# Taking the gathered expert slots of a unit in the order 0, 8, 1, 9 and so on

## The chip, the cores and the metric

The kernel runs on one core of a Trainium2 chip. Its engines are TensorE (PE, with its weight loads shown as PEld), VectorE (DVE), ScalarE (ACT), GpSimd (POOL) and SyncE (SP, which only issues DMAs). Each engine takes its own instructions in order and waits on semaphores. Sixteen DMA engines move data between the chip's memory (HBM) and the on-chip memory (SBUF). The metric is the device time of one execution in microseconds, as the median of the runs shown: 3331.66 us for the kernel before, from three runs between 3331.08 and 3334.54 us.

## The reference, cut to what matters

The reference computes two transformer blocks on 256 tokens of width 2048, in float32. The change lies in one part of the second block, a mixture of 16,384 tiny experts. Each of 8 heads of a token picks its 16 best experts. For each of them the row `u` is multiplied with the token, a gelu is taken, and the row `v` is added to the token's output with that weight:

```
top_s, top_i = lax.top_k(s, PEER_TOPK)                 # PEER_TOPK = 16, per half of the key
cand = top_s[..., 0, :, None] + top_s[..., 1, None, :]
best_s, best_c = lax.top_k(cand, PEER_TOPK)            # best first
experts = i1 * N_KEYS + i2
gates = jax.nn.softmax(best_s, axis=-1)
...
u = peer_u[ec]
act = jax.nn.gelu(jnp.einsum('tkd,td->tk', u, xc))
return jnp.einsum('tk,tkd->td', gc * act, peer_v[ec])
```

The 16 experts of a head are sorted, the best first, so their gates fall with the rank. With the inputs used here many gates of the later ranks are so small that the softmax gives zero in float32.

## The kernel before, in words

Nearly all of the program is dense matrix products whose weights stream in from HBM. The part in question, `peer` (L1318), stands between the second block's attention and recurrence and its last gated layer (`ple`).

*Units and slots.* The 256 tokens are cut into four blocks of 64 (`u`), the 8 heads into four pairs (`g`). A **unit** is one (`u`, `g`): partitions 0 to 63 hold the 64 tokens for the first head of the pair, partitions 64 to 127 the same tokens for the second. There are 16 units, and a unit has 16 **slots**, 256 in all. Slot `j` of a unit does this (`slot`, L1385):

- POOL issues one indirect DMA (L1389), which gathers into a buffer `uvb` one row per partition, 4096 floats (16 KiB): the expert's `u` row and `v` row, as the list `idx[:, j]` names them. An index beyond the table is skipped, and its row isn't fetched.
- DVE multiplies the `u` half with the tokens and sums (L1393, a SCALAR_TENSOR_TENSOR and the read of its accumulator).
- ACT takes the gelu, multiplies by the gate, and makes a diagonal matrix `dgs` (L1394 to L1397).
- PE multiplies that with the `v` half and adds it into `acc_e` (L1402).

There are six buffers `uvb` (`UVB`), used in turn. The gather of slot n+6 is issued when PE has read the buffer of slot n. DVE, ACT and PE take the slots in the order in which they are issued.

*The lists.* `route` (L1419) makes the 16 expert numbers and gates per partition for one unit, almost all on DVE. At its end it adds a large number to each expert number whose gate is zero, so that the gather skips that row. It also swaps the list's halves for partitions 64 to 127 (L1474): column `j` holds rank `j` in partitions 0 to 63, and rank `j`+8, or `j`-8 from column 8 on, in partitions 64 to 127. So slots 0 to 7 take the first head's ranks 0 to 7 beside the second head's ranks 8 to 15, and slots 8 to 15 the other way round. For unit 0 the first six columns (L1480 to L1482) get their expert numbers without skips, so that every buffer is filled once.

*The order of the work.* In `peer` the loop over slots calls `slot` and after every second one advances the next unit's `route` by a step; `route` has six such steps. The program text is not the order on an engine: a scheduler of the language places each engine's instructions by what it estimates, and it lets the routing run up to four units ahead (the lists have four buffers). On DVE the routing stands in bursts: most of units 1 to 4's in unit 0, and then one unit's at the turn of each unit, until the last unit's is done in unit 9.

The following lines are the functions that the change touches.

## Time and profile before

| | us |
|---|---|
| median of the runs | 3331.66 |
| the profiled execution | 3339.52 |
| its span, first to last instruction | 3337.8 |
| L1393 on DVE, 256 slots, busy | 586.3 |
| L1402 on PE, 256 slots, busy | 590.3 |
| L1389 on POOL, 256 gathers, busy | 432.6 |

The profile is one execution. Busy times are sums over an engine's instructions. A line of instructions shows how often it ran, its busy time, the mean of one, and the idle time of the engine just before it with the work that ended that idle time. Units are counted from 0, in the order (`u`, `g`). The slots run from 2253.3 us (the first gather's issue) to 3221.5 us (the last slot's matmuls end). Before and after them the program is dense products.

### The profile page before, as it was taken

How to read it: one execution, taken by the hardware profiler on the slowest of the kernel's cores; microseconds unless marked ns; L12 is line 12 of the kernel's file. 1: busy time of each engine (PE TensorE's matmuls, PEld its weight loads, DVE VectorE, ACT ScalarE, POOL GpSimd, SP SyncE). 2: the span in 40 equal slices, each digit the busy share in tenths (PEclk: the TensorE clock that was granted, in tenths of full speed). 3: DMA queues.
4: the chain of work that ended last, by engine and by line, in shares of the span. 5: the costliest groups of instructions: out<-in, count | busy, mean ns of one | idle time of the engine just before them, and what ended most of it. 6: DMA issues, size and time to landing. Idle time of an engine off the chain costs nothing. (4 is left out here: it accounts for less than half of the span.)

```text
span 3337.8 us, 45840 instructions
## 1 busy us (share of the span) xinstructions
PE 2918.3 (87%) x17372; PEld 2274.2 (68%) x17372; DVE 2165.0 (65%) x3087; ACT 1439.5 (43%) x2464; POOL 545.6 (16%) x320
## 2 busy tenths in 40 slices
PE   8999999999999999999999999985556666666678
PEld 8888888989898989999999998881111111111136
DVE  7769675545555555875445677559777867776755
ACT  5446655434343445664434445433222323222234
POOL 0000000000000000010000110003453444454511
PEclk9999999999999999999999999997897788899979
DMA  7645564666666666556665446637767767777864
GB/s 255 182 149 185 165 182 145 186 190 186 191 183 195 183 189 189 166 183 184 183 183 171 144 156 215 184 114 281 279 253 291 276 258 269 291 289 294 309 234 144
DMA packets 156397, 693.14 MB, mean 208 GB/s; under 512 B 34049, under 2 KB 36353, under 8 KB 139777
## 3 DMA queue, kind: packets, MB, share of 16 engines
q1 hardware_dynamic: 119312, 425.64, 41.8%
q0 software_dynamic: 36864, 264.57, 21.1%
q8 instruction: 137, 2.24, 0.3%
q14 instruction: 84, 0.69, 0.1%
HBM read 955.12 MB, written 4.19 MB: 287 GB/s over the span
## 5 line engine op out<-in xcount | busy, mean ns | idle before, releaser
L1402 PE MATMUL acc_e<-uvb,dgs 128*64 128x512 f32 x2048 | 590.3, 708 | 363.3 <-ACT dgs L1397 363.1
L1393 DVE SCALAR_TENSOR_TENSOR f<-uvb,xg 128x2048 bf16<-128x2048 f32 x256 | 586.3, 2290 | 229.2 <-DMA uvb<-in_uv,idx 219.2
L1402 PEld LDWEIGHTS acc_e<-uvb,dgs 128*64 128x64 f32 x2048 | 141.8, 154 | 801.8 <-ACT dgs L1397 610.3
L1389 POOL DMA_INDIRECT uvb<-in_uv,idx x256 | 432.6, 1690 | 753.7 <-PE acc_e L1402 408.8
L1394 ACT ACTIVATE act<-act 128x1 f32<-128x1 f32 x256 | 51.9, 203 | 638.6 <-DVE f L1393 638.5
L381 PE MATMUL acc_w_up<-f,l_w_up 128*128 128x256 f32 x1024 | 289.9, 283 | 0.0
L378 PE MATMUL acc_w_up<-f,h_w_up 128*128 128x256 f32 x1024 | 289.8, 283 | 0.0
L380 PE MATMUL acc_w_up<-f,h_w_up 128*128 128x256 f32 x1024 | 289.8, 283 | 0.0
L362 DVE TENSOR_TENSOR l_w_up<-r_w_up,h_w_up 128x1024 fp32r<-128x1024 f32 x128 | 165.8, 1295 | 175.7 <-PE acc_w_up L381 153.2
L362 DVE TENSOR_TENSOR l_w_down<-r_w_down,h_w_down 128x1024 fp32r<-128x1024 f32 x128 | 161.3, 1260 | 162.1 <-PE acc_w_down L372 133.4
L361 ACT CAST h_w_down<-r_w_down 128x1024 fp32r<-128x1024 f32 x128 | 135.1, 1055 | 197.8 <-PE acc_w_down L373 168.6
L361 ACT CAST h_w_up<-r_w_up 128x1024 fp32r<-128x1024 f32 x128 | 134.9, 1054 | 196.4 <-PE acc_w_up L380 175.4
L371 PE MATMUL acc_w_down<-h_w_down,f 128*128 128x512 f32 x512 | 199.6, 390 | 0.0
L372 PE MATMUL acc_w_down<-l_w_down,f 128*128 128x512 f32 x512 | 199.5, 390 | 0.0
L373 PE MATMUL acc_w_down<-h_w_down,f 128*128 128x512 f32 x512 | 199.2, 389 | 0.0
L380 PEld LDWEIGHTS acc_w_up<-f,h_w_up 128*128 128x128 f32 x1024 | 196.6, 192 | 0.1
L378 PEld LDWEIGHTS acc_w_up<-f,h_w_up 128*128 128x128 f32 x1024 | 196.6, 192 | 0.1
L381 PEld LDWEIGHTS acc_w_up<-f,l_w_up 128*128 128x128 f32 x1024 | 196.6, 192 | 0.0
L584 POOL TENSOR_TENSOR f<-f 128x1024 f32<-128x1024 f32 x16 | 30.3, 1896 | 802.7 <-ACT f L583 802.7
L373 PEld LDWEIGHTS acc_w_down<-h_w_down,f 128*128 128x128 f32 x512 | 96.1, 188 | 19.9
L372 PEld LDWEIGHTS acc_w_down<-l_w_down,f 128*128 128x128 f32 x512 | 96.1, 188 | 19.8
L371 PEld LDWEIGHTS acc_w_down<-h_w_down,f 128*128 128x128 f32 x512 | 96.1, 188 | 19.7
(555 smaller groups left out, 7818.0 us busy)
## 6 DMA issues: line engine op xcount, KB each, us to landing
r_w_up<-in_w_up SPq DMA_DIRECT2D x128, 512.0 KB, 3.7
r_w_down<-in_w_down SPq DMA_DIRECT2D x128, 512.0 KB, 4.2
r_w_qkv<-in_w_qkv SPq DMA_DIRECT2D x48, 512.0 KB, 3.6
r_w_xbc<-in_w_xbc SPq DMA_DIRECT2D x32, 512.0 KB, 4.5
r_w_xr<-in_w_xr SPq DMA_DIRECT2D x32, 512.0 KB, 3.6
r_w_yr<-in_w_yr SPq DMA_DIRECT2D x32, 512.0 KB, 3.6
r_w_gr<-in_w_gr SPq DMA_DIRECT2D x32, 512.0 KB, 3.6
r_w_ro<-in_w_ro SPq DMA_DIRECT2D x32, 512.0 KB, 3.7
```

Of the source, the lines that this page charges most:

```text
L361: nc.scalar.copy(wh, raw)
L362: nc.vector.tensor_sub(wl, raw, wh.bitcast(F32))
L371: nc.tensor.matmul(o, xh[:, s], h, start=first, stop=False)
L372: nc.tensor.matmul(o, xh[:, s], l, start=False, stop=False)
L373: nc.tensor.matmul(o, xl[:, s], h, start=False, stop=fin)
L378: nc.tensor.matmul(o, wh[:, s], xh, start=first and b % 2 == 0, stop=False, skip_group_check=True)
L380: nc.tensor.matmul(o, wh[:, s], xl, start=False, stop=False, skip_group_check=True)
L381: nc.tensor.matmul(o, wl[:, s], xh, start=False, stop=fin, skip_group_check=True)
L1389: nc.gpsimd.indirect_dma_start(out=b, out_offset=None, in_=self.ap["uv"], in_offset=bass.IndirectOffsetOnAxis(ap=idx[:, j:j + 1], axis=0), ...
L1393: nc.vector.scalar_tensor_tensor(junk, b[:, :D], 1.0, xg, op0=ALU.mult, op1=ALU.mult, accum_out=a[:, 0:1])
L1394: nc.scalar.activation(a[:, 2:3], a[:, 0:1], AF.Gelu_apprx_tanh)
L1402: nc.tensor.matmul(acc[i * 64:(i + 1) * 64, c * 512:(c + 1) * 512], dg, b[:, o:o + 512], start=first, stop=last)
```

## The change

The loop takes the columns of the list in the order 0, 8, 1, 9, 2, 10 and so on to 7, 15. Lists, gates, gathered rows and sums stay the same except in the very first six gathers. `first` and `last`, which open and close PE's accumulation, follow the place in the loop (`begin`, `end`). The steps of the next unit's `route` are called after places 0, 1, 3, 4, 6 and 7. In the first unit the six columns without skips are now 0 to 2 and 8 to 10, which takes four small casts in place of two.

```diff
+            order = [r + 8 * i for r in range(8) for i in range(2)]
...
-                for j in range(16):
-                    self.slot(u, g, j, uv[slot % UVB], xg[u], junk, acc[u])
+                for k, j in enumerate(order):
+                    self.slot(u, g, j, uv[slot % UVB], xg[u], junk, acc[u], k == 0, k == 15)
                     slot += 1
-                    if j % 2:
+                    if k in (0, 1, 3, 4, 6, 7):
                         next(later, None)
-                    if g == 0 and j == 2 and u:
+                    if g == 0 and k == 2 and u:
                         self.block_out(u - 1, acc[u - 1])
-                    if i == 15 and j in (3, 6, 9, 12):
-                        if j == 3:
+                    if i == 15 and k in (3, 6, 9, 12):
+                        if k == 3:
...
-        first, last = g == 0 and j == 0, g == 3 and j == 15
+        first, last = g == 0 and begin, g == 3 and end
...
-            nc.vector.tensor_copy(idx[0:64, :UVB], ids[0:64, 0, :UVB])
-            nc.vector.tensor_copy(idx[64:128, :UVB], ids[64:128, 0, 8:8 + UVB])
+            k = UVB // 2
+            for p, o in ((0, 0), (64, 8)):
+                nc.vector.tensor_copy(idx[p:p + 64, 0:k], ids[p:p + 64, 0, o:o + k])
+                nc.vector.tensor_copy(idx[p:p + 64, 8:8 + k], ids[p:p + 64, 0, 8 - o:8 - o + k])
```

How the instructions stand on an engine is shown at two places. The first is DVE at the start of unit 2 (`u` 0, `g` 2), in the kernel before; `act0_2_8` is the sum of slot column 8 of that unit, `tv`, `bc` and `tiu` are routing of later units:

```order
L1393 SCALAR_TENSOR_TENSOR f4_301_21719,act0_2_1_22286<-uvb3_21716,xg0_21709 128x2048
L1490 MAX tv23_24515<-sc23_24513 128x8 x2
L1491 MAX_INDEX bc21_24038<-best21_24037,cand21_24035 128x8
L1491 MAX_INDEX tiu23_24516<-tv23_24515,sc23_24513 128x8 x2
L1393 SCALAR_TENSOR_TENSOR f4_301_21719,act0_2_2_22314<-uvb4_21717,xg0_21709 128x2048
L1393 SCALAR_TENSOR_TENSOR f4_301_21719,act0_2_3_22327<-uvb5_21718,xg0_21709 128x2048
L1393 SCALAR_TENSOR_TENSOR f4_301_21719,act0_2_4_22346<-uvb0_21713,xg0_21709 128x2048
L1393 SCALAR_TENSOR_TENSOR f4_301_21719,act0_2_5_22359<-uvb1_21714,xg0_21709 128x2048
```

The same place on DVE in the changed kernel (its lines are numbered higher by up to three):

```order
L1394 SCALAR_TENSOR_TENSOR f4_301_21721,act0_2_8_22303<-uvb3_21718,xg0_21711 128x2048
L1493 MAX tv23_24504<-sc23_24502 128x8 x2
L1494 MAX_INDEX bc21_24014<-best21_24013,cand21_24011 128x8
L1494 MAX_INDEX tiu23_24505<-tv23_24504,sc23_24502 128x8 x2
L1394 SCALAR_TENSOR_TENSOR f4_301_21721,act0_2_1_22322<-uvb4_21719,xg0_21711 128x2048
L1394 SCALAR_TENSOR_TENSOR f4_301_21721,act0_2_9_22335<-uvb5_21720,xg0_21711 128x2048
L1394 SCALAR_TENSOR_TENSOR f4_301_21721,act0_2_2_22360<-uvb0_21715,xg0_21711 128x2048
L1394 SCALAR_TENSOR_TENSOR f4_301_21721,act0_2_10_22383<-uvb1_21716,xg0_21711 128x2048
```

The columns change, and the routing stays between the same places: from unit 1 on, each gap between two slots holds the same number of routing instructions in both kernels. Only unit 0 differs. There DVE in the kernel before has 16 routing instructions between the first two slots, 16 before the third and 12 before the fourth; the end of the first gap is this (`mr286`, `eq02` and `ex02` are routing):

```order
L1456 TENSOR_TENSOR eq020_22139<-ab02_22133,cst_75 128x256
L1456 TENSOR_TENSOR eq021_22169<-ab02_22133,cst_75 128x256
L1467 RECIPROCAL s286_22201<-s286_22201 128x1
L1492 MATCH_REPLACE mr286_22305<-tv03_22303,sc03_22301 128x128
L1393 SCALAR_TENSOR_TENSOR f4_301_21719,act0_0_1_21738<-uvb1_21714,xg0_21709 128x2048
L1458 TENSOR_TENSOR eq020_22139<-eq020_22139,tif02_22095 128x256
L1458 TENSOR_TENSOR eq021_22169<-eq021_22169,tif02_22095 128x256
L1468 TENSOR_SCALAR ex02_22199<-ex02_22199,s286_22201 128x16
```

In the changed kernel DVE has 39 there, then 2 and 5; the end of the first gap, with the next three slots:

```order
L1494 MAX_INDEX tiu11_22846<-tv11_22845,sc11_22843 128x8 x2
L1496 MAX best03_22349<-mr288_22351 128x8
L1394 SCALAR_TENSOR_TENSOR f4_301_21721,act0_0_8_21755<-uvb1_21716,xg0_21711 128x2048
L1497 MAX_INDEX bc03_22350<-best03_22349,mr288_22351 128x8
L1464 TENSOR_TENSOR ex03_22423<-best03_22349 128x16
L1394 SCALAR_TENSOR_TENSOR f4_301_21721,act0_0_1_21774<-uvb2_21717,xg0_21711 128x2048
L1451 TENSOR_SCALAR au03_22371<-bc03_22350 128x16
L1452 TENSOR_SCALAR au03_22371<-bc03_22350 128x16
L1467 TENSOR_REDUCE s290_22425<-ex03_22423 128x1
L1453 CAST ab03_22370<-au03_22371 128x32
L1468 RECIPROCAL s290_22425<-s290_22425 128x1
L1394 SCALAR_TENSOR_TENSOR f4_301_21721,act0_0_9_21787<-uvb3_21718,xg0_21711 128x2048
```

Routing that stood between the second and the fourth slot now stands between the first and the second; by the fourth slot the two sums are 44 and 46 instructions.

## Rows read from the trace of the kernel before

**Rows 1.** Page, costliest groups: line, shapes, count | busy us, mean ns | idle before, releaser.
```profile
L1402 PE MATMUL acc_e<-uvb,dgs 128*64 128x512 f32 x2048 | 590.3, 708 | 363.3 <-ACT dgs L1397 363.1
L1393 DVE SCALAR_TENSOR_TENSOR f<-uvb,xg 128x2048 bf16<-128x2048 f32 x256 | 586.3, 2290 | 229.2 <-DMA uvb<-in_uv,idx 219.2
L1389 POOL DMA_INDIRECT uvb<-in_uv,idx x256 | 432.6, 1690 | 753.7 <-PE acc_e L1402 408.8
```
**Rows 2.** Windows: unit 0, units 1 to 8, units 9 to 15: busy us, clock, DMA share, GB/s.
```profile
2261.54:2343.66 82.12, 46.17 (x168) 13.64 (x168) 80.68 (x272) 30.92 (x77) 30.03 (x16) 0.79 0.71 276
2343.66:2837.68 494.02, 302.22 (x1056) 74.60 (x1056) 373.38 (x627) 145.15 (x464) 217.11 (x129) 0.85 0.74 271
2837.68:3216.25 378.57, 244.91 (x884) 59.59 (x886) 261.20 (x248) 98.81 (x346) 179.04 (x106) 0.88 0.75 285
```
**Rows 3.** Line L1393 in units 1 to 8: count, ns min/median/max; DVE's idle by releaser.
```profile
L1393 DVE SCALAR_TENSOR_TENSOR f<-uvb,xg x128: 2271/2292/2307, 2343.7 to 2831.0; 128x2048 bf16<-128x2048 f32 x128
...
  DMA uvb<-in_uv,idx: 111.3, 66
```
**Rows 4.** Line L1393 in units 9 to 15: the same.
```profile
L1393 DVE SCALAR_TENSOR_TENSOR f<-uvb,xg x112: 2279/2293/2334, 2837.7 to 3216.2; 128x2048 bf16<-128x2048 f32 x112
...
  DMA uvb<-in_uv,idx: 107.3, 75
```
**Rows 5.** DMA queues of the page: packets, MB, share of 16 engines.
```profile
q0 software_dynamic: 36864, 264.57, 21.1%
```
**Rows 6.** Windows: the first gathers, a routing burst, and the last gathers.
```profile
2262.00:2285.00 23.00, 11.31 (x38) 3.44 (x40) 22.80 (x85) 9.89 (x22) 6.06 (x3) 0.72 1.01 430
3197.00:3216.00 19.00, 12.44 (x32) 2.65 (x30) 8.91 (x8) 3.38 (x12) 0.00 (x0) 0.60 0.24 96
...
2460.00:2476.00 16.00, 6.93 (x24) 1.51 (x22) 15.26 (x52) 6.17 (x16) 4.27 (x3) 0.89 0.54 213
```
**Rows 7.** DVE's timeline at the last slots: start us, us, instruction, idle before.
```profile
3201.62 2.29 DVE L1393 SCALAR_TENSOR_TENSOR f<-uvb,xg 128x2048 bf16<-128x2048 f32 x1 [2.61 <-DMA uvb<-in_uv,idx]
...
3216.25 2.29 DVE L1393 SCALAR_TENSOR_TENSOR f<-uvb,xg 128x2048 bf16<-128x2048 f32 x1 [2.58 <-DMA uvb<-in_uv,idx]
```
**Rows 8.** DVE's timeline in unit 2 and at the start of unit 3.
```profile
2417.72 2.29 DVE L1393 SCALAR_TENSOR_TENSOR f<-uvb,xg 128x2048 bf16<-128x2048 f32 x1
...
2420.05 2.29 DVE L1393 SCALAR_TENSOR_TENSOR f<-uvb,xg 128x2048 bf16<-128x2048 f32 x1
...
2431.21 2.29 DVE L1393 SCALAR_TENSOR_TENSOR f<-uvb,xg 128x2048 bf16<-128x2048 f32 x1 [1.86 <-DMA uvb<-in_uv,idx]
...
2459.65 2.29 DVE L1393 SCALAR_TENSOR_TENSOR f<-uvb,xg 128x2048 bf16<-128x2048 f32 x1 [1.36 <-DMA uvb<-in_uv,idx]
...
2475.76 2.27 DVE L1393 SCALAR_TENSOR_TENSOR f<-uvb,xg 128x2048 bf16<-128x2048 f32 x1
```
**Rows 9.** DVE's timeline before the first gather, one of the casts of L1481 and L1482.
```profile
2251.86 0.16 DVE L1481 CAST idx<-ids 64x6 uint32<-64x6 f32 x1
```
**Rows 10.** POOL's timeline in unit 2: gathers issued while DVE runs slot on slot.
```profile
2423.51 2.03 POOL L1389 DMA_INDIRECT uvb<-in_uv,idx  x1 [0.30 <-issue]
2425.84 2.03 POOL L1389 DMA_INDIRECT uvb<-in_uv,idx  x1 [0.30 <-issue]
...
2430.51 0.99 POOL L1389 DMA_INDIRECT uvb<-in_uv,idx  x1 [0.30 <-issue]
```
**Rows 11.** Line L1389, all gathers: ns min/median/max; us from issue to landing.
```profile
L1389 POOL DMA_INDIRECT uvb<-in_uv,idx x256: 984/1576/3105, 2253.3 to 3195.9; - x128
...
DMA to landing us min/median/max: 5.8/14.0/26.1
```

## The prediction

> **What bounds the kernel now.** The slots take 954.7 us, from the first to the last DVE slot, and only they are touched. I read the costliest groups first [rows 1]. L1393 is 256 slots of 2.29 us on DVE, and of the 229.2 us that DVE idled ahead of them 219.2 were ended by a gather that landed. PE waits for ACT, ACT follows DVE, POOL waits for PE to free a buffer: these follow from DVE's pace. So DVE and the gathers are the two candidates.

> Next I read windows by stretch [rows 2] with DVE's waits in each [rows 3, 4]. In unit 0 DVE is busy 80.7 of 82.1 us (routing): the gathers don't matter there. Units 1 to 8 take 494.0 us, 61.75 each: 46.7 DVE work, 13.9 waiting for gathers, 1.2 other. The 111 slots of units 9 to 15 (6.94 units, the last slot left out) take 378.6 us, 54.6 per unit: 37.7 work, 15.5 waiting, 1.5 other. Yet the DMA engines are busy only 0.74 and 0.75 of these stretches. Gathers are late while a quarter of the DMA engines' time is idle.

> Two windows show how [rows 6]. The first gathers fetch all 128 rows, share 1.01 at 430 GB/s: 128 x 16 KiB in 4.88 us, 8 rows for each of 16 DMA engines at 0.61 us. At the last slots DVE's starts also lie 4.88 us apart (3201.62 to 3216.25 in three steps, each start waiting for a gather) [rows 7], but the share is 0.24. So at least one DMA engine has 8 live rows in every gather while most have nearly none.

> Which rows are live follows from the reference: counted on its inputs, 15,777 of 32,768 gates are not zero. This fits the bytes: 264.57 MB are 16,148 rows of 16 KiB [rows 5], some 370 of them forced in the first six gathers. By rank, 0 to 15, the live shares are 1.00, .95, .88, .78, .68, .60, .51, .43, .37, .33, .27, .23, .20, .18, .15, .13. In the kernel before, slots 8 to 15 give partitions 64 to 127 the ranks 0 to 7 (8 x 5.83 = 46.7 rows per eight partitions) and the others 14.9; slots 0 to 7 do the reverse. If each half of the partitions has its own DMA engines, half of them wait for the other half, twice a unit. Unit 2 fits: slots 9 to 15 should take 8 x 4.83 x 0.61 = 23.6 us on an average engine of the loaded half, and took 28.4 (2431.21 to 2459.65) [rows 8], 1.20 times that.

> No row names the engine of a partition. [...]

> **The change part by part.** *The order of the columns.* Each two slots now hold ranks r and r+8 for both halves. The rows of an engine over a unit stay the same: 15,777 / 256 = 61.6 on average, 37.6 us. What counts is the heaviest engine. It is at least 1.20 times the mean (unit 2 above, 45.1 us) and at most 1.45 times, since in units 9 to 15 its unchanged rows fit into 54.6 us. I take 1.3, between the ends, as no row is nearer to either: 49 us a unit. Eight pairs then cost 6.34 us (8 x 0.61 x 1.3) times 1.37, 1.28, 1.15, 1.01, .88, .78, .66 and .56: from 8.7 us for the first down to 3.6 for the last.

> Units 9 to 15: DVE needs 2.33 us a slot (2417.72 to 2420.05) [rows 8], 4.66 a pair, which is more than the last two pairs' 4.2 and 3.6; this adds 1.5, so 50.5 in place of 54.6 us. 4.1 x 6.94 is a gain of 28 us. What is late next there: gathers in the first five pairs, DVE at the end.

> Units 1 to 8: DVE alone needs 46.7 + 1.2 = 47.9. Its routing stands at the turn of the unit, 16.1 us from slot 15 to the next unit's slot 2 (2459.65 to 2475.76) [rows 8]; meanwhile up to six heavy gathers land unseen. The last four pairs now need 18.4 us of DMA beside 18.6 of DVE, so the waits that stood at slots 8 to 15 go. But a burst also holds buffers back: in 2460 to 2476 the share fell to 0.54 from 0.75 [rows 2, 6], 16 x 0.21 = 3.4 us of DMA time. 49 + 3.4 = 52.4 in place of 61.75 us, a gain of 9.35 x 8 = 75 us.

> *The casts.* Two more of 0.16 us ahead of the first gather [rows 9]: 0.3 us.

> *The routing steps.* From unit 1 on routing stands in the same gaps on DVE, so the new call places are worth nothing there. In unit 0 DVE does 23 routing instructions more before its second slot; unit 0's average 0.18 us (80.7 less 16 x 2.29, over 272 - 32 instructions) [rows 1, 2], so that slot is some 4 us late, and the fourth only 2 instructions, 0.4 us. The gather that waits for that slot's buffer comes later by as much, hidden by unit 0's DVE work; uncovered it would be 4 us. The first six gathers also fetch 78 rows fewer (counted as above), 3 us of DMA under the same cover: nothing.

> *All else* (PE, ACT, the DMAs on SP, the block sums) is issued in the same order and number.

> Sum: 75 + 28 less 0.7 is 102 us. The profiled execution takes 3339.5 us (span 3337.8); it would take 3237. The median lies 7.9 us lower, so I forecast 3230.

> **The rivals.** *DVE becomes the bound*: the six buffers even out the engines and all 219 us of waits go, 3113 us; two thirds to all of it is 3113 to 3186. For it: the DMA share of 0.75. Against: single engines stay full for long, as at the end, where five gathers took 24.4 us at a mean of 8 x 3.0 x 0.61 = 14.7 for the loaded half, 1.66 times it.

> *POOL becomes the bound.* Issuing a gather takes 0.99 us by itself but 2.03 while DVE runs slot on slot [rows 10], and up to 3.1 [rows 11]. If denser DVE work made all of them 3.1 + 0.3, a unit would take 54.4: units 9 to 15 gain nothing, units 1 to 8 gain 7.3 each, 59 in all, 3273 us. Against: at 2.03 + 0.30 POOL keeps exactly DVE's 2.33. [...]

> *The heaviest engine is at 1.45*: units 9 to 15 stay at 54.6, units 1 to 8 go to 54.6 + 3.4 = 58, a gain of 30, 3302 us.

> *Slower*: rows are spread evenly over the DMA engines, and lateness comes from a gather's own 14.0 us to landing [rows 11]. Before, both halves of a unit then load the DMA alike, 18.8 us beside DVE's 18.6. Now the first eight slots have 38.5 rows an engine (23.5 us), the last eight 23.1 (14.1 us, DVE's 18.6 rule): 42.1 in place of 37.6, 4.5 more in each of the last seven units, 31 in all, 3363 us; in units 1 to 8 the routing covers it. It decides as soon as the loaded and the idle half of a gather share engines. Against it stands the share of 0.24 at full-length gathers.

> *It does nothing that counts*: the waits come back elsewhere, within 0.2% (6.7 us), about what a measurement can tell.

> **How the numbers follow.** My forecast, 3186 to 3260, has 0.66; DVE as the bound 0.10; POOL 0.10; ratio 1.45 0.07; slower 0.04; nothing 0.03. That is 0.93 faster, 0.03 the same, 0.04 slower. The range of 3180 to 3295 holds the forecast, POOL's case and an edge of DVE's, some 0.8; its ends are gains of 152 and 37 us, between no waits at all and ratio 1.45.

> **What would show it.** Right: DVE's waits for gathers fall from 219 to about 115 us; units 1 to 8 take about 420 us, units 9 to 15 about 350; the waits at slots 8 to 15 of units 1 to 8 go, and those left in units 9 to 15 stand in the first ten slots; the share over units 9 to 15 rises from 0.75 to above 0.8; the last gathers come closer than 4.88 us. Wrong: starts 4.88 us apart at a low share also in the changed kernel (the halves weren't the cause, or one engine stays the bound); L1389 well above its 1.69 us on average with POOL idle for little (POOL); DVE without waits (its bound); a gain in unit 0.

## The result, and the profile after

| | before | after |
|---|---|---|
| median of the runs, us | 3331.37 (3329.36 to 3334.54, 4 runs) | 3240.38 (3237.30 to 3248.76, 4 runs) |
| ratio | | 0.973, 95% interval 0.9709 to 0.9751 |
| profiled execution, us | 3339.52 | 3243.22 |
| first to last DVE slot, us | 954.7 | 860.4 |
| DVE's waits for gathers, us | 219.2 | 122.4 |

The change saves 91 us. In the profiles it is 96.3 us, and the stretch of the slots gives 94.3 of them.

The costliest groups of the changed kernel, whose lines answer to those of [rows 1]:

```profile
L1403 PE MATMUL acc_e<-uvb,dgs 128*64 128x512 f32 x2048 | 554.0, 672 | 303.5 <-ACT dgs L1398 303.5
L1394 DVE SCALAR_TENSOR_TENSOR f<-uvb,xg 128x2048 bf16<-128x2048 f32 x256 | 586.5, 2291 | 136.6 <-DMA uvb<-in_uv,idx 122.4
L1390 POOL DMA_INDIRECT uvb<-in_uv,idx x256 | 431.6, 1686 | 669.3 <-PE acc_e L1403 319.5
```

DVE does the same 256 slots in the same busy time. What shrank is its wait for landings, from 219.2 to 122.4 us. POOL's issue of a gather is unchanged, 1.69 us. The windows of unit 0, units 1 to 8 and units 9 to 15, as in [rows 2] (busy us and counts of PE, PEld, DVE, ACT and POOL, then granted clock, DMA share, GB/s):

```profile
2260.54:2342.26 81.72, 46.04 (x168) 13.81 (x168) 80.43 (x271) 30.91 (x77) 26.53 (x16) 0.73 0.68 263
2342.26:2771.20 428.94, 280.79 (x1056) 71.27 (x1056) 373.85 (x628) 145.18 (x464) 218.18 (x129) 0.90 0.84 310
2771.20:3120.97 349.77, 229.40 (x880) 58.29 (x880) 261.08 (x247) 98.64 (x346) 180.55 (x106) 0.94 0.83 311
```

Unit 0 stays, units 1 to 8 lose 65.1 us and the last stretch 28.8 us, at the same DVE work. The DMA share rises from 0.74 and 0.75 to 0.84 and 0.83. The waits for gathers in units 1 to 8 (first line) and units 9 to 15 (second), as in [rows 3, 4], read on L1394:

```profile
  DMA uvb<-in_uv,idx: 42.6, 42
```

```profile
  DMA uvb<-in_uv,idx: 79.0, 63
```

Most of what went lay in units 1 to 8 (111.3 before). DVE's timeline of the last slots shows what became of the starts 4.88 us apart [rows 7]:

```profile
3106.25 2.29 DVE L1394 SCALAR_TENSOR_TENSOR f<-uvb,xg 128x2048 bf16<-128x2048 f32 x1
...
3109.99 2.29 DVE L1394 SCALAR_TENSOR_TENSOR f<-uvb,xg 128x2048 bf16<-128x2048 f32 x1 [1.44 <-DMA uvb<-in_uv,idx]
...
3112.38 2.29 DVE L1394 SCALAR_TENSOR_TENSOR f<-uvb,xg 128x2048 bf16<-128x2048 f32 x1
...
3115.52 2.29 DVE L1394 SCALAR_TENSOR_TENSOR f<-uvb,xg 128x2048 bf16<-128x2048 f32 x1 [0.84 <-DMA uvb<-in_uv,idx]
...
3120.97 2.29 DVE L1394 SCALAR_TENSOR_TENSOR f<-uvb,xg 128x2048 bf16<-128x2048 f32 x1 [0.77 <-DMA uvb<-in_uv,idx]
```

Five steps take 14.7 us, 2.94 each. Every second slot still waits. These are columns 13, 14 and 15, which give partitions 64 to 127 the ranks 5, 6 and 7. So one half of the partitions, as it seems, has the longer lists in this unit, but its engines get a light gather in between.

### The profile page after: what moved, and what is told of

It reads as the page before. It is cut to its first block, busy times and chain, and to the rows that moved or that the text cites. A ratio compares the mean times of both kernels' runs of the same rounds, so it can differ in the third digit from the quotient of the medians.

```text
span 3241.5 us, 45843 instructions
## 1 busy us (share of the span) xinstructions
PE 2879.1 (89%) x17372; PEld 2268.3 (70%) x17372; DVE 2164.7 (67%) x3089; ACT 1438.7 (44%) x2464; POOL 544.7 (17%) x320
## 5 line engine op out<-in xcount | busy, mean ns | idle before, releaser
L1403 PE MATMUL acc_e<-uvb,dgs 128*64 128x512 f32 x2048 | 554.0, 672 | 303.5 <-ACT dgs L1398 303.5
L1394 DVE SCALAR_TENSOR_TENSOR f<-uvb,xg 128x2048 bf16<-128x2048 f32 x256 | 586.5, 2291 | 136.6 <-DMA uvb<-in_uv,idx 122.4
L1403 PEld LDWEIGHTS acc_e<-uvb,dgs 128*64 128x64 f32 x2048 | 138.2, 149 | 710.1 <-ACT dgs L1398 523.7
L1390 POOL DMA_INDIRECT uvb<-in_uv,idx x256 | 431.6, 1686 | 669.3 <-PE acc_e L1403 319.5
```

The lines of the kernel that those rows point to most:

```text
L1390: nc.gpsimd.indirect_dma_start(out=b, out_offset=None, in_=self.ap["uv"], in_offset=bass.IndirectOffsetOnAxis(ap=idx[:, j:j + 1], axis=0), ...
L1394: nc.vector.scalar_tensor_tensor(junk, b[:, :D], 1.0, xg, op0=ALU.mult, op1=ALU.mult, accum_out=a[:, 0:1])
L1403: nc.tensor.matmul(acc[i * 64:(i + 1) * 64, c * 512:(c + 1) * 512], dg, b[:, o:o + 512], start=first, stop=last)
```

## The experiments

All times are medians; each ratio is to the kernel before, run on the same chip. "Units 1 to 8", "units 9 to 15" and DVE's waits for gathers are read from each run's one profiled execution, with windows as above.

| run | us | ratio, 95% interval | units 1 to 8 | units 9 to 15 | DVE's waits |
|---|---|---|---|---|---|
| order alone | 3241.5 | 0.9729, 0.9716 to 0.9742 | 433.7 | 347.3 | 125.7 |
| routing steps alone | 3332.9 | 1.0004, 0.9993 to 1.0015 | 488.7 | 376.5 | 212.0 |
| light pairs first | 3299.6 | 0.9911, 0.9896 to 0.9926 | 471.9 | 356.4 | 176.1 |
| flat order | 3253.5 | 0.9770, 0.9757 to 0.9784 | 442.7 | 344.8 | 131.6 |
| partitions 64 to 127 cut | 3220.4 | 0.9667, 0.9648 to 0.9686 | 413.6 | 336.7 | 98.5 |
| p % 8 of 4 to 7 cut | 3196.0 | 0.9594, 0.9574 to 0.9614 | 402.8 | 324.4 | 66.0 |
| odd partitions cut | 3128.6 | 0.9392, 0.9371 to 0.9413 | 386.1 | 273.2 | 0.4 |
| odd cut, old order | 3135.0 | 0.9411, 0.9339 to 0.9483 | 386.4 | 273.2 | 1.1 |
| no swap | 3285.1 | 0.9863, 0.9846 to 0.9879 | 450.3 | 370.8 | 169.9 |
| mixed orders | 3243.8 | 0.9721, 0.9708 to 0.9734 | 432.4 | 345.8 | 120.2 |
| two list buffers | 3233.7 | 0.9692, 0.9679 to 0.9706 | 434.6 | 349.4 | 112.6 |
| five gather buffers | 3300.5 | 0.9902, 0.9887 to 0.9917 | 458.2 | 371.7 | 176.7 |

**Which part of the change does it.** First the new order with the old places of the routing steps:

```diff
-                    if k in (0, 1, 3, 4, 6, 7):
+                    if k % 2:
                         next(later, None)
```

> The new column order, with the routing steps called after every second slot as before. Theory (each half of the partitions has its own DMA engines, and the order alone evens them): 3240 us within 7, DVE's waits for gathers near 122 us as in the changed kernel. Rival (the earlier routing steps carry the gain): 3331 us, waits near 219 us.

Then the old order with the new places:

```diff
-                    if j % 2:
+                    if j in (0, 1, 3, 4, 6, 7):
                         next(later, None)
```

> The old column order 0 to 15, with the routing steps called after places 0, 1, 3, 4, 6 and 7. Theory: 3331 us within 7, waits near 219 us, and single gathers at the end still 4.88 us apart at a DMA share near 0.24. Rival (routing steps): 3240 us.

The order alone gives 3241.5 us, the steps alone 3332.9. The order is the whole effect. The new places of the calls are worth nothing, since the scheduler puts the routing where it did: in both traces every engine's instructions stand in the same order as in the changed kernel (order alone) and as in the kernel before (steps alone).

So the two runs also repeat those kernels, and show what one profile is worth. Units 1 to 8 took 428.9 and 433.7 us in the new order, 494.0 and 488.7 in the old, units 9 to 15 349.8 and 347.3, 378.6 and 376.5. A difference of some 5 us between two windows says nothing below.

At the end of the second kernel gathers came 4.9 us apart again (DVE's starts at 3192.25, 3197.11, 3202.00 and 3206.87 us). The DMA share was 0.32 in the 19 us up to 3206, where I had expected 0.24.

**Whether the halves have their own engines.** Three kernels fetch half of the rows, each by another mask. The gate below which a row is skipped becomes a column per partition:

```diff
+    put("thr", np.where(i >= 64, 2.0, TINY)[:, None])      # or i % 8 >= 4, or i % 2 == 1
...
-        nc.vector.tensor_scalar(z, ex, TINY, float(4 * N_EXPERTS), op0=ALU.is_lt, op1=ALU.mult)
+        nc.vector.tensor_scalar(z, ex, self.c("thr"), float(4 * N_EXPERTS), op0=ALU.is_lt, op1=ALU.mult)
```

> The changed kernel, but in partitions 64 to 127 no row is fetched after the first six gathers (their sums are left wrong): half of the rows go. Theory (partitions 64 to 127 have DMA engines of their own, eight partitions each): the loaded engines keep their rows, the heaviest has 81 in place of 84 a unit, 49.5 us, so the time falls by 0 to 40 us, to 3200 to 3240, at a DMA share near half of 0.83. Rival (rows are spread evenly over all 16 engines): the DMA work per engine halves, DVE's waits all but go, 3120 to 3140 us.

> The changed kernel, but no row is fetched for partitions with p % 8 of 4 to 7: again half of the rows go. [...] Rival (an engine has eight neighbouring partitions): every engine's rows halve, heaviest 46 a unit, 28.2 us, below DVE's pace: waits all but gone, 3120 to 3140 us.

> The changed kernel, but no row is fetched for odd partitions: again half of the rows go. Theory (either map by blocks of partitions): every engine's rows halve, heaviest 47 a unit, 28.7 us, below DVE's 39 to 48 us a unit: DVE's waits for gathers fall from 122 us to under 15, 3120 to 3140 us. Rival (neighbouring partitions go to different engines in turn): eight engines keep all rows, 51 us a unit, 3220 to 3240 us. This also tells whether DVE's pace is what lies under the waits.

And the third mask in the kernel before:

> The kernel before (old column order), but no row is fetched for odd partitions after the first six gathers, so every DMA engine's rows halve. Theory (the orders differ only through the loaded half's DMA engines): the loaded half then needs 33 us / 2 = 17 us in eight slots, less than DVE's 18.6, so the old order costs nearly nothing any more: DVE's waits for gathers under 25 us, 3125 to 3150 us, within 20 of the same cut in the new order (3129). Rival (the old order holds something else back, such as landings or buffers): 60 to 90 us above 3129.

The windows of units 1 to 8 and 9 to 15, first with partitions 64 to 127 cut:

```profile
2344.92:2758.52 413.60, 282.10 (x1056) 71.36 (x1056) 373.54 (x628) 145.15 (x464) 215.46 (x128) 0.88 0.45 164
2758.52:3095.18 336.66, 231.06 (x880) 58.58 (x880) 261.21 (x247) 98.06 (x344) 178.34 (x106) 0.93 0.43 164
```

Then with p % 8 of 4 to 7 cut:

```profile
2343.54:2746.33 402.79, 273.60 (x1056) 69.85 (x1056) 373.48 (x628) 145.16 (x464) 230.55 (x128) 0.92 0.45 162
2746.33:3070.77 324.44, 221.45 (x880) 56.14 (x880) 261.17 (x246) 98.02 (x344) 191.02 (x106) 0.96 0.43 160
```

Then with the odd partitions cut:

```profile
2343.77:2729.83 386.06, 274.78 (x1056) 69.79 (x1056) 373.40 (x627) 145.19 (x464) 239.52 (x128) 0.91 0.57 178
2729.83:3002.99 273.16, 215.40 (x880) 54.54 (x880) 261.15 (x246) 98.06 (x344) 213.71 (x106) 0.98 0.62 199
```

And with the odd partitions cut in the old order:

```profile
2344.52:2730.87 386.35, 271.99 (x1056) 68.87 (x1056) 373.42 (x627) 145.16 (x464) 240.46 (x128) 0.92 0.54 178
2730.87:3004.05 273.18, 215.38 (x880) 54.54 (x880) 261.18 (x247) 98.08 (x344) 213.81 (x106) 0.98 0.59 200
```

**Where in a unit the heavy gathers stand.** Two more orders of the same pairs; the forced columns of unit 0 follow them:

```diff
-            order = [r + 8 * i for r in range(8) for i in range(2)]
+            order = [r + 8 * i for r in range(7, -1, -1) for i in range(2)]          # light first
+            order = [r + 8 * i for r in (0, 7, 1, 6, 2, 5, 3, 4) for i in range(2)]  # flat
```

> Halves as even as in the changed kernel, but the pairs run from ranks 7 and 15 to 0 and 8, so that each unit's light gathers come first. If evenness of the halves is the whole effect: 3240 us within 7. If it also matters that six heavy gathers land under the routing burst at a unit's start: the first three pairs then hold only some 13 us of DMA work beside a burst of 16.1, so units 1 to 8 take 3 to 5 us more each (429 to some 460 us in all), units 9 to 15 stay within 10 of 350, and the time is near 3270. Rival (the rows are spread evenly over the engines, only the steepness of the load counts): units 9 to 15 as in the changed kernel, no statement on the burst.

> Pairs in the order of ranks 0, 7, 1, 6, 2, 5, 3, 4 (each with its rank plus 8): the halves are even and any four slots carry about the same load. Theory: the heaviest engine's sum over a unit is unchanged, so units 9 to 15 gain only the 1.5 us each that DVE's pace adds to the light pairs at the end (350 to some 340 us), units 1 to 8 stay within 10 of 429: 3225 to 3240 us. If the steep fall within a unit costs much more than that, below 3210.

Evenness of the halves isn't all. With light pairs first, 59 of the 91 us go again (3299.6 less 3240.4); in the profiles it is 49.8 us, 42.9 of them in units 1 to 8, where the bursts are, and 6.7 in units 9 to 15. The 16 us after slot 15 of unit 2, a routing burst, in the changed kernel (the kernel before had a share of 0.54 there [rows 6]):

```profile
2439.30:2455.30 16.00, 8.13 (x28) 2.04 (x28) 15.27 (x52) 6.62 (x18) 6.04 (x5) 0.76 0.95 388
```

The same 16 us with light pairs first:

```profile
2451.10:2467.10 16.00, 7.07 (x24) 1.65 (x22) 15.26 (x52) 6.17 (x16) 4.13 (x3) 0.77 0.42 156
```

DVE is equally busy, but the DMA engines move 388 GB/s under the burst in the one and 156 in the other. Over the eight bursts at the turns from unit 0 to unit 8 the share averages 0.93 in the changed kernel, 0.81 in the flat order and 0.56 with light pairs first. Among these three, whose halves are even, units 1 to 8 take the longer the lower that share is, 429, 443 and 472 us. The kernel before (0.68 and 494 us) doesn't fit in, as its halves are uneven. I had expected 460 us for light pairs first, and 3270 in all: the direction was right, the size too small. The flat order costs 14 us in units 1 to 8, where at most 10 were expected, and gains 5 in units 9 to 15, no more than two profiles of one kernel can differ by, where 10 were expected. Its total, 3253.5, lies above the range.

**Without the swap of the list's halves.**

```diff
-            order = [r + 8 * i for r in range(8) for i in range(2)]
+            order = list(range(16))
...
-        for p, n, src, dst in ((0, 64, 0, 0), (64, 64, 0, 8), (64, 64, 8, 0)):
-            w = 16 if p == 0 else 8
+        for p, n, src, dst in ((0, 128, 0, 0),):
+            w = 16
```

> The list's halves aren't swapped and the columns go 0 to 15, so slot j holds rank j in both halves: halves even, but a gather's load falls from 8 rows an engine to 1 over the unit. Theory (evenness of the halves first, heavy gathers under the burst second): the heaviest engine's sum over a unit stays; units 9 to 15 lose some, as the last eight slots go at DVE's 18.6 us and the first eight cost 34 to 37, 52 to 55 a unit (about 370 us in all); units 1 to 8 near 429. 3240 to 3275 us, clearly below 3331. Rival (what counts is that each gather has the same number of rows, which the swap was for): slower than the kernel before, above 3340 us.

3285.1 us: well under the kernel before (3329.9 on that chip), though a gather's load now falls from 8 rows an engine to 1. That each gather carry the same number of rows is worth less than that each engine does. Units 9 to 15 came as expected (370.8), units 1 to 8 were expected near 429 and took 450.3. The time went over the range by 10 us. A unit's first six gathers then hold 39 live rows an engine on average by the counted gates, 24 us by estimate (8 rows in the 4.88 us of a full gather [rows 6]), more than a burst of 16 us covers. The trace fits this. The burst after unit 2 again:

```profile
2440.88:2456.88 16.00, 8.01 (x28) 2.03 (x28) 15.35 (x50) 6.35 (x16) 6.11 (x5) 0.74 1.01 430
```

All DMA engines are full there (1.01), and over the eight bursts the share averages 1.00. Yet in units 1 to 8 49.9 of the 67.1 us of waits then stand at slots 0 to 7, right behind the bursts, where the changed kernel has 13.3. So a high share under the burst isn't enough: what doesn't land under it is waited for. No run changed this alone.

**Buffers and lists.** Five gather buffers in place of six:

```diff
-UVB = 6
+UVB = 5
```

> The changed kernel with five gather buffers in place of six. Theory: what the buffers do is to let heavy gathers run ahead under a routing burst and to bridge from engine to engine. Under the burst of 16.1 us five gathers still hold some 20 us of DMA work, but the loop through five buffers (issue, landing, DVE, ACT, PE) has less time: units 1 to 8 rise by 1 to 4 us each, units 9 to 15 by 1 to 3: 3255 to 3295 us. If the heaviest engine's sum alone sets the unit: within 7 of 3240.

3300.5 us, just above the range: one buffer is worth some 60 us here, as much as light pairs first. Units 1 to 8 rise by 3.7 us each and units 9 to 15 by 3.2, though the bursts' DMA share stays at 0.91. So the heaviest engine's sum doesn't set the time by itself. Seven buffers were not run.

Then a version with the orders mixed, which was to beat the change:

```diff
-                for k, j in enumerate(order):
+                for k, j in enumerate(order if i < 9 else flat):
```

> A version meant to beat both: the changed kernel's order in units 0 to 8, where the routing bursts stand, and the flat order of the earlier experiment in units 9 to 15, where there are none. Theory (heavy gathers first pay only under a burst): units 1 to 8 as in the changed kernel, near 429 us, units 9 to 15 as in the flat one, near 345: 3235 us, 5 below the changed kernel, at the edge of what can be measured. Rival (the 5 us were chance): 3240 us.

3243.8 us. Units 9 to 15 take 345.8, as in the flat order, but units 1 to 8, in the same order as the changed kernel, 432.4. Both windows lie within what two profiles of one kernel differ by, and the ratio, 0.9721, is that of the order alone (0.9729). No gain is shown.

And two buffers for the lists, so that less routing is done ahead:

```diff
-        idx = stg.tile([P, 16], U32, tag="idx", bufs=4, name=f"idx{nm}")
-        gate = stg.tile([P, 16], F32, tag="gate", bufs=4, name=f"gate{nm}")
+        idx = stg.tile([P, 16], U32, tag="idx", bufs=2, name=f"idx{nm}")
+        gate = stg.tile([P, 16], F32, tag="gate", bufs=2, name=f"gate{nm}")
```

> The changed kernel with two buffers for the lists and gates in place of four, so that DVE does 107 routing instructions in unit 0 in place of 173 and the bursts go on to unit 11. Theory (unit 0 waits for DVE alone, later units for the heaviest DMA engine): unit 0 falls by 66 x 0.18 = 12 us to some 70; units 9 to 11 get bursts and cost up to 3.6 us more each, as units 1 to 8 do over 9 to 15: 3229 to 3240 us. Rival (a burst is hidden wholly under gathers): 3228 us. Rival (routing closer to its use makes gathers wait for their list): above 3245 us.

Its windows:

```profile
2259.59:2328.15 68.56, 41.21 (x152) 11.56 (x152) 64.29 (x181) 23.54 (x63) 28.73 (x16) 0.75 0.81 322
2328.15:2762.71 434.56, 283.11 (x1072) 72.92 (x1072) 375.64 (x642) 145.88 (x466) 232.90 (x128) 0.90 0.83 305
2762.71:3112.12 349.41, 234.58 (x880) 58.86 (x880) 275.94 (x323) 105.13 (x358) 180.74 (x106) 0.92 0.82 310
```

Unit 0 falls by 13.2 us, as DVE does 181 instructions in it in place of 271. In units 9 to 15 DVE works 14.9 us more in the same time: there the routing lies wholly under gathers, as the first rival had it for these units, and not at the up to 3.6 us a unit that I had put. Units 1 to 8 take 5.6 us more than in the changed kernel, about what two profiles differ by. 3233.7 us is the fastest of the kernels that fetch all rows; its interval to the kernel before (0.9679 to 0.9706) lies just under the changed kernel's (0.9709 to 0.9751). The two weren't timed against each other.

## Why the prediction was right, point by point

- *The halves wait for each other.* Shown: by the order alone (3241.5), by the masks (98.5 us of waits left without partitions 64 to 127, 0.4 without the odd ones), and by the old order losing nothing once the engines are unloaded (743 us over the slots in both orders).
- *Units 9 to 15, 50.5 us each.* Measured 349.8 / 6.94 = 50.4. I put 49 us for the heaviest engine, at 1.3 times the mean, and 1.5 for DVE's pace in the light pairs. The 1.3 is an estimate between 1.20 and 1.45. No run shows it, nor the rows of the heaviest engine that the expectations of the masks use (84, 81 and 47 a unit): they need the engine of each partition, which was not shown. What the runs show in their place are a unit's times, 50.4 us with nothing cut, 48.5 without partitions 64 to 127 and 39.4 without the odd ones. The flat order, which should save the 1.5, saved 0.7, too little to tell from nothing. So the total of 50.5 is right, but its parts aren't shown.
- *Units 1 to 8, 52.4 us each.* Measured 53.6. Here a step failed: that "a burst also holds buffers back", put at 3.4 us from a share of 0.54. In the changed kernel the burst is where the DMA engines do best, 0.95 at the start of unit 3 and 0.93 on average (0.56 with light pairs first), because the six buffers then hold the unit's heaviest gathers; my own sentence before it, that heavy gathers land unseen, was the stronger half. What raises the average are two units: 4 takes 65.7 us and 8 takes 58.0, the others 49.1 to 54.1. Both in the changed kernel, 4 first, and then unit 4 alone with partitions 64 to 127 cut and with p % 8 of 4 to 7 cut:

```profile
2495.47:2561.21 65.74, 37.48 (x128) 8.81 (x128) 49.89 (x95) 19.41 (x57) 22.84 (x17) 0.87 0.86 303
2713.23:2771.20 57.97, 38.13 (x144) 10.58 (x144) 53.50 (x103) 25.70 (x80) 27.91 (x17) 0.85 0.83 287
```

```profile
2491.91:2554.16 62.25, 38.56 (x128) 9.12 (x128) 49.90 (x95) 19.40 (x57) 22.98 (x17) 0.81 0.48 169
```

```profile
2491.90:2543.43 51.53, 33.94 (x128) 8.24 (x128) 49.81 (x95) 19.40 (x57) 33.41 (x17) 0.93 0.48 166
```

In unit 8 DVE is busy for 53.5 of the 58.0 us, and with odd partitions cut the unit still takes 56.3: that is DVE's own work there, among it 4.7 us of the last gated layer's norm (16 instructions of L310). Unit 4 takes 51.3 with odd partitions cut: its waits go with the rows of partitions with p % 8 of 4 to 7, and stay with those of 0 to 63. Which engines those rows load isn't shown. So 3.4 was about the right size by luck, for a wrong reason.
- *Waits left.* 122.4 us, forecast some 115. Added up by a slot's place in its unit, 101.9 of the 111.3 us in units 1 to 8 stood at slots 8 to 15 before; of those 29.3 are left, so they shrank and did not go. In units 9 to 15 62.7 of the 79.0 us stand in the first ten slots, as forecast. The next two had 8.0, as the forecast's own sixth pair, 0.78 x 6.34 = 4.9 us, is above DVE's 4.66 too.
- *Casts, routing steps, unit 0: nothing.* Unit 0 went from 82.1 to 81.7 us, and the steps alone gave a ratio of 1.0004. Two readings were off. The routing that moved in unit 0 moves with the order, not with the calls: it does so by the order alone, and not by the steps alone. And the 23 are rows of a listing in which one row can be several instructions; in the traces 57 instructions stand before the second slot in place of 24, which starts 12.9 us after the first in place of 6.7, so 6.2 us later and not 4. Unit 0's routing covered that as well.
- *The rivals.* DVE as the bound: a floor of 743 us over the slots, seen with odd partitions cut; the change stops 118 us above it. POOL: the mean issue stayed 1.69 us, and rose to 1.92 only with odd partitions cut, where DVE's waits for gathers were gone all the same. A ratio of 1.45: too high, as units 9 to 15 took 50.4 us each and not 54.6. Even spread, slower: excluded by the masks.

The forecast of a gain of 102 us was made against the profiled execution, and the profiles differ by 96.3. Units 1 to 8 gave 9.9 less than forecast (65.1 for 75), units 9 to 15 0.8 more, unit 0 1.1 more (0.4 gained where 0.7 was to be lost), and 2.0 came outside the slots. By the medians it is 91.0, since the profiled execution of before lies 8.1 us above its median and that of after 2.8.

## What to carry to other kernels

When a transfer is late while the DMA share is well under one, look for engines that are idle in the same moment: here a share of 0.24 while gathers took the 4.88 us of a full one [rows 6, 7] went with a few engines carrying them. Even out the load per DMA engine over the transfers in flight. In these gathers it went by partition (98.5 and 66.0 us of waits left with the first two masks, 0.4 with the third); an even load per transfer mattered less (3285.1 us without it, 3329.9 before). And put the heaviest transfers where the consumer is busy with something else (3240.4 us with heavy pairs first, 3299.6 with light ones), but no more of them than that time covers: without the swap the share under the bursts was 1.00, and 49.9 us of waits stood right behind them.

## What the runs showed of the hardware that had not been expected

- The granted clock in units 1 to 8 rose from 0.85 to 0.90 of the full clock and in units 9 to 15 from 0.88 to 0.94, while the same matmuls stood closer together; the mean of one in L1402 (after: L1403) fell from 708 to 672 ns. What that gave isn't shown apart: POOL's gathers wait for PE to free a buffer (319.5 us of POOL's idle time).
- Where DVE had nothing to wait for, POOL's issue of a gather was longer (mean 1.92 us with odd partitions cut in the old order, 1.69 in the kernel before), but gathers were in time all the same.
